# A triangular solve moved into the attention of a hybrid layer, and its successor's preparation spread over the projections

## The chip, the cores and the metric

The kernel runs on one core of one Trainium2 chip. The metric is the device time of one execution in microseconds (us). A core has several engines, each with its own queue of instructions, which meet through semaphores: TensorE (PE; its weight loads are listed as PEld), VectorE (DVE), ScalarE (ACT), GpSimd (POOL) and SyncE (SP), which here issues the DMAs.

## The reference, cut to what matters

One layer of a diffusion backbone over 512 latent tokens with 256 context tokens ahead of them, model width 1024, in float32. One input projection feeds two branches: softmax attention (8 query heads, 2 key heads) and a bidirectional chunked gated DeltaNet (8 heads, two directions, chunks of 64). The branches are gated, merged and projected; a gated MLP with a short convolution follows. The change concerns the triangular solve of the DeltaNet branch:

```python
gam = jnp.cumsum(log_a, axis=-1)
dec = jnp.exp(jnp.where(incl, gam[..., :, None] - gam[..., None, :], -jnp.inf))
kk = jnp.einsum('bhncd,bhnsd->bhncs', k, k)
a_mat = jnp.where(strict, beta[..., :, None] * dec * kk, 0.0) + jnp.eye(GDN_CHUNK)
uw = lax.linalg.triangular_solve(a_mat, rhs, left_side=True, lower=True, unit_diagonal=True)
...
def step(s, inp):
    delta = u_c - jnp.einsum('bhcd,bhde->bhce', w_c, s)
    s_new = gl_c[..., None, None] * s + jnp.einsum('bhcd,bhce->bhde', kd_c, delta)
    o = jnp.einsum('bhcd,bhde->bhce', qd_c, s) + jnp.einsum('bhcs,bhse->bhce', p_c, delta)
```

## The kernel before

Activations lie transposed, channels on the 128 partitions and tokens along the free axis. Every projection is a float32 product built from three matmuls: a weight block of 128 x 1024 is loaded (`wraw`), split into a high part on ACT (`whi`) and the rest on DVE (`wlo`), and multiplied with the high and low parts of the activations (`hxH`, `hxL` for latent tokens, `hcH`, `hcL` for context). The sums stand in two PSUM banks (`mb`); a third bank (`xb`) serves transposes, a pair (`ab`) and a large bank (`pS`) the attention.

The stages in the order of the trace: modulation vectors (to 50 us), key, value and query projections (to 153), attention (to 325), fill steps with the first DeltaNet pair's preparation and solve (to 428), the stages of the four DeltaNet pairs with their scans (to about 800), then gated merge, output projection and MLP (to the end), in which PE has hardly a pause.

*Attention.* `attend()` runs 32 units (8 heads x 4 blocks of 128 queries) plus two to drain. A unit takes scores, softmax, transposes of the probabilities, and the product with the values. Between its parts it takes steps of `fillA`, the projections of the DeltaNet's keys and values for the first heads; each of their results passes through the short convolution (taps on DVE into `t`, then `co`, an ACT tanh and a DVE product), is transposed through `xb`, scaled by `hk`, and stored to DRAM as `kTd`, `ktd` or `vtd`. The normalising factors of a head, `rkk` and `hk`, end in a power taken on POOL.

*DeltaNet pairs.* The 8 heads go in four pairs p = 0 to 3. `gdn_prep(p)` loads the keys `kT`, broadcasts `gamdr` into the decay tiles `NN` and `Gb`, adds the mask, takes 24 Exps on ACT (one per chunk, direction and head) and adds the two directions. `gdn_solve` multiplies these with the grams of the keys (PE into the single bank `pk`), gathers the 32 x 32 diagonal blocks into `C` (DVE transposes and ACT copies), turns them into `X`, and solves all blocks at once in 31 rows of two operations, a product `prod` and an addition to `R`. `gdn_solved` scales R by the rates `gT` and transposes it into `o_tr` and `o_nt`. `gdn_inv(p)` builds the full inverses from these on PE, and `gdn_scan(p)` does the recurrence. For p = 0 the 31 rows run on DVE, for the others on POOL.

*What sets the order.* From the attention's end on, PE's instructions stand in the order of the code (pinned); the other engines' instructions are placed by a scheduler with priorities (`sooner`, `solver`, `first`, `early`). `filler()` yields steps of projection work, and `weave(g, rate)` takes so many of them for each step of g. The code ahead of the first scan is 24 fill steps (`WK`), the first solve, 66 fill steps (`W0`), and the inverses with 2.4 fill steps to each of theirs:

```python
weave(wait(WK), 1.0)
weave(gdn_solve(pre, G if 0 in SPOOL else V), RK)
gdn_solved(pre, False)
weave(wait(W0), 1.0)
```

Helpers record most operations: in the profile L86 is a matmul, L90 a transpose on PE, L107 a tensor-tensor operation, L111 a tensor-scalar one, L116 a scalar-tensor-tensor one, L119 an activation.

Of the kernel before, what the change touches and what calls it, by code (L numbers as in the profile page):

```python
# [6 lines left out]
F32 = mybir.dt.float32  # L7
F32R = mybir.dt.float32r
AF = mybir.ActivationFunctionType
ALU = mybir.AluOpType  # L10
# [21 lines left out]
CHUNK, WK, W0, W1, RI, RS, RO = 1, 24, 66, 0, 3.0, 2.8, 2.0  # L32
# [45 lines left out]
def hybrid_layer_body(tc, x, ctxt, xT, consts, cols, rows, w_mod1, w_mod2, w_av, w_aq, w_cm, w_pa, w_pd, w_out,  # L78
# [26 lines left out]

    def tt(out, a, b, op, eng=None):
        (eng or V).tensor_tensor(out=out, in0=a, in1=b, op=op)  # L107

    def ts(out, a, s1, op0, s2=None, op1=None, eng=None):
        if op1 is None:  # L110
            (eng or V).tensor_scalar(out=out, in0=a, scalar1=s1, scalar2=None, op0=op0)  # L111
        else:
            (eng or V).tensor_scalar(out=out, in0=a, scalar1=s1, scalar2=s2, op0=op0, op1=op1)  # L113

    def stt(out, a, s, b, op0, op1):
        V.scalar_tensor_tensor(out=out, in0=a, scalar=s, in1=b, op0=op0, op1=op1)  # L116

    def act(out, a, f=AF.Copy, **kw):
        A.activation(out, a, f, **kw)  # L119
# [13 lines left out]
    with es:  # L133
# [89 lines left out]
        vtd = [dp.tile([P, NA], F32, name=f"vtd{i}") for i in range(NH)]  # L223
        szd = [dp.tile([P, NL], F32, name=f"szd{i}") for i in range(NH)]
# [445 lines left out]
        QH = [ap_.tile([P, 2, NL], F32R, name=f"QH{i}") for i in range(4)]  # L670
        QL = [ap_.tile([P, 2, NL], F32R, name=f"QL{i}") for i in range(4)]
# [90 lines left out]
        with at_es:  # L762
# [62 lines left out]

            def attend():
                U = 4 * NH
                at = lambda u: (u // 4, u % 4)
                pS, pms, pv = scores(0, 0), {}, None
                yield F0  # L830
                for u in range(U + 2):
                    if u < U:
                        pms[u] = softmax(*at(u), pS)
                    if u + 1 < U:
                        pS = scores(*at(u + 1))
                    yield F1
# [40 lines left out]
        def gdn_prep(p, eng=G):  # L877
# [25 lines left out]
            return [kT, gT, NN]  # L903

# [292 lines left out]

        with early():
            pre = gdn_prep(0, V if P0 else G)
# [3 lines left out]
        def filler():  # L1203
# [95 lines left out]
        count = [0.0]  # L1299

        def weave(g, rate):
            for w in g:
                count[0] += rate * (w or 1)
                while count[0] >= 1.0:
                    count[0] -= 1.0
                    next(fill, None)
# [14 lines left out]
        weave(gdn_solve(pre, G if 0 in SPOOL else V), RK)  # L1321
        gdn_solved(pre, False)
# [8 lines left out]
        for p in range(NP):  # L1331
            cur = pre
            pre = gdn_prep(p + 1) if p + 1 < NP else None
            g = stage(p, cur, pre)
            weave(g, RI if p else RI0)
            while not gpool or len(ready) < 2 * p + 2:
                next(fill)
# [273 lines left out]
```

## Time and profile before

| | us |
|---|---|
| median of three runs | 1258.49 |
| the three runs | 1258.39, 1258.49, 1265.28 |
| the profiled execution | 1256.38 |
| its span in the trace | 1254.5 |

The profiled execution's time is 1.9 over its span. The profile gives it in 40 slices of 31 us; each digit is the busy share in tenths:

```profile
PE   7999999999889899899999999899999999999996
DVE  5767767777698866766757687855776766653333
ACT  6634466766675673773634632233544444442231
POOL 0120110110422387597484200210000000000000
```

The attention ends in the eleventh slice. POOL has little to do up to there; in the three or four slices behind it DVE and ACT are at their fullest and PE falls to 8. The rest of the profile is read in the prediction.

### The profile page before, as it was taken

The numbers are of one execution on the slowest core, as the hardware profiler recorded it, in microseconds if no ns is written. First come the engines' busy times: TensorE is split into PE (matmuls) and PEld (weight loads), VectorE is DVE, ScalarE is ACT, GpSimd is POOL, SyncE is SP. The second block draws the span as 40 slices with busy tenths as digits, with TensorE's granted clock in tenths as the row PEclk, the third lists the DMA queues.
The fourth block names the chain that finished last, engine by engine and source line by source line (L and its number), as shares of the span: only waits on it lengthen the run. The fifth ranks groups of instructions, "written<-read, shape, count | busy, mean of one in ns | idle before, by whom it ended". The sixth has DMA issues, their size and how long they took to land. (4 is left out here: it accounts for less than half of the span.)

```text
span 1254.5 us, 20509 instructions
## 1 busy us (share of the span) xinstructions
PE 1196.7 (95%) x7733; PEld 1018.3 (81%) x7733; DVE 837.4 (67%) x1609; ACT 613.8 (49%) x1403; POOL 274.0 (22%) x347
## 2 busy tenths in 40 slices
PE   7999999999889899899999999899999999999996
PEld 3599879898778788778888778679888888888886
DVE  5767767777698866766757687855776766653333
ACT  6634466766675673773634632233544444442231
POOL 0120110110422387597484200210000000000000
PEclk9999999999999999999999999999999999999999
DMA  9412311211634533643546786854343332233331
GB/s 377 145 60 85 103 43 60 80 68 60 214 110 162 179 119 115 171 140 107 174 143 192 239 295 210 272 194 135 96 136 122 133 101 101 88 93 96 102 93 67
DMA packets 66403, 171.83 MB, mean 137 GB/s; under 512 B 7328, under 2 KB 18048, under 8 KB 64896
## 3 DMA queue, kind: packets, MB, share of 16 engines
q1 hardware_dynamic: 66304, 170.52, 41.0%
q8 instruction: 61, 1.00, 0.3%
q14 instruction: 38, 0.31, 0.1%
HBM read 145.28 MB, written 25.21 MB: 136 GB/s over the span
## 5 line engine op out<-in xcount | busy, mean ns | idle before, releaser
L107 DVE TENSOR_TENSOR wlo<-wraw,whi 128x1024 fp32r<-128x1024 f32 (+1 forms) x153 | 192.2, 1257 | 155.7 <-ACT whi L119 155.5
L119 ACT ACTIVATE whi<-wraw 128x1024 fp32r<-128x1024 f32 (+1 forms) x153 | 159.6, 1044 | 219.3 <-PE mc L86 112.5
L86 PE MATMUL mc<-h,whi 128*128 128x512 f32 (+1 forms) x752 | 219.7, 376 | 0.3 <-ACT whi L119 0.3
L86 PE MATMUL mb<-hxH,whi 128*128 128x512 f32 x384 | 162.3, 423 | 3.4 <-DVE R L107 2.8
L86 PEld LDWEIGHTS mc<-h,whi 128*128 128x128 f32 x752 | 138.0, 188 | 25.8 <-ACT whi L119 0.5
L86 PE MATMUL mb<-hxH,wlo 128*128 128x512 f32 x384 | 152.6, 397 | 0.0
L86 PE MATMUL mb<-hxL,whi 128*128 128x512 f32 x384 | 151.7, 395 | 0.0
L86 PE MATMUL mc<-h,wlo 128*128 128x512 f32 (+1 forms) x376 | 141.4, 376 | 0.5 <-DVE wlo L107 0.5
L86 PE MATMUL mc<-a,whi 128*128 128x512 f32 (+1 forms) x396 | 111.1, 367 | 0.6 <-DVE x L116 0.6
L107 POOL TENSOR_TENSOR rc<-rc,mhalf 128x2 f32<-128x2 f32 x4 | 3.3, 813 | 407.5 <-DVE rc L113 407.5
L86 PEld LDWEIGHTS mb<-hxH,wlo 128*128 128x128 f32 x384 | 72.9, 190 | 16.5
L86 PEld LDWEIGHTS mb<-hxH,whi 128*128 128x128 f32 x384 | 73.5, 191 | 13.7 <-issue 2.9
L86 PEld LDWEIGHTS mc<-h,wlo 128*128 128x128 f32 x376 | 70.8, 188 | 13.8 <-DVE wlo L107 1.0
L86 PEld LDWEIGHTS mc<-a,whi 128*128 128x128 f32 x396 | 71.6, 189 | 12.8 <-DVE x L116 0.8
L86 PEld LDWEIGHTS mb<-hxL,whi 128*128 128x128 f32 x384 | 73.5, 191 | 9.6
L86 PE MATMUL mc<-a,wlo 128*128 128x512 f32 (+1 forms) x198 | 72.4, 366 | 0.0
L116 DVE SCALAR_TENSOR_TENSOR u<-mc,col,u 128x511 f32<-128x511 f32 x88 | 65.3, 746 | 1.4
L107 POOL TENSOR_TENSOR prod<-X,R 128x31 f32<-128x31 f32 (+15 forms) x93 | 54.4, 584 | 20.6 <-DVE X L107 13.9
L107 POOL TENSOR_TENSOR R<-R,prod 128x31 f32<-128x31 f32 (+15 forms) x93 | 57.1, 614 | 7.0
L86 PE MATMUL pq<-whi,hxH 128*128 128x256 f32 (+1 forms) x192 | 55.6, 290 | 0.0
L86 PE MATMUL pq<-wlo,hxH 128*128 128x256 f32 (+1 forms) x192 | 54.4, 283 | 0.1
L86 PE MATMUL pq<-whi,hxL 128*128 128x256 f32 (+1 forms) x192 | 54.3, 283 | 0.0
(329 smaller groups left out, 2768.1 us busy)
## 6 DMA issues: line engine op xcount, KB each, us to landing
wraw<-in_w_cm_dram SPq DMA_DIRECT2D x48, 512.0 KB, 3.6
wraw<-in_w_up_dram SPq DMA_DIRECT2D x44, 512.0 KB, 3.3
wl<-in_w_mod_dram SPq DMA_DIRECT2D x24, 512.0 KB, 4.6
wm<-in_w_mod_dram SPq DMA_DIRECT2D x8, 1024.0 KB, 10.7
wraw<-in_w_down_dram SPq DMA_DIRECT2D x16, 512.0 KB, 3.5
wraw<-in_w_aq_dram SPq DMA_DIRECT2D x10, 512.0 KB, 3.7
M<-gamdr SPq DMA_DIRECT2D x64, 64.0 KB, 4.9
wraw<-in_w_pa_dram SPq DMA_DIRECT2D x8, 512.0 KB, 4.4
```

What stands on the lines that cost most here:

```text
L86: i = nc.tensor.matmul(*a, **k)
L107: (eng or V).tensor_tensor(out=out, in0=a, in1=b, op=op)
L116: V.scalar_tensor_tensor(out=out, in0=a, scalar=s, in1=b, op0=op0, op1=op1)
L119: A.activation(out, a, f, **kw)
```

## The change

The first pair's masks, decays, grams, blocks and solve are taken out of the code behind the attention and cut into pieces. A generator `first_solve()` yields them, and `solve_pieces(u)`, called in each unit of the attention, takes pieces worth one credit a unit (`S0R`), none before the unit that a piece names. All of a piece's instructions are pinned into the program's order on their engines (`in_order`, `put`). The 31 rows stand in unit 20 with no credit, on POOL; the scaling by gT stands in unit 32, on POOL too. The tiles take the places of query tiles that are no longer needed (QH and QL become one tag `Q` with four buffers), so the results go to DRAM: `nnd` (the masked grams) and `rrd` (R). `gdn_first()` loads them again, with kT.

Behind the attention there are 8 fill steps (`WK`), the two transposes `o_tr` and `o_nt` (pinned), 12 fill steps (`W0`), and the first pair's inverses. The second pair's preparation and solve become `gdn_pieces(1)`, cut in the same way; `side_pieces` takes from them half a credit (`SRA`) with each fill step. Its masks and rows are on POOL. The fill steps take the query and z projections of two heads as q, q, z, z in place of q, z, q, z. The number of matmuls is unchanged.

```diff
-CHUNK, WK, W0, W1, RI, RS, RO = 1, 24, 66, 0, 3.0, 2.8, 2.0
+S0E, S0R, SRA = 0, 1, .5
+CHUNK, WK, W0, W1, RI, RS, RO = 1, 8, 12, 0, 3.0, 2.8, 2.0
...
+    def put(i):
+        return tc.keep_in_program_order(i) if strict[0] else i
...
-        QH = [ap_.tile([P, 2, NL], F32R, name=f"QH{i}") for i in range(4)]
-        QL = [ap_.tile([P, 2, NL], F32R, name=f"QL{i}") for i in range(4)]
+        QQ = [ap_.tile([P, 2, 2, NL], F32R, name="Q", tag="Q", bufs=4) for _ in range(4)]
+        QH, QL = ([q[:, i] for q in QQ] for i in range(2))
...
+                def masks(D, d, hh):
+                    tc.keep_in_program_order(SP.dma_start(
+                        D.rearrange("p a b -> p (a b)"),
+                        gamdr[rows6(d, hh), :].rearrange("a b -> (a b)").partition_broadcast(P)))
+                    tt(D, D, msk_s[d].unsqueeze(1).to_broadcast([P, 6, P]), ALU.add, G)
...
+                def gram(hh, c0, n):
+                    pb = xbank()
+                    for i in range(n):
+                        sl = slice((c0 + i) * P, (c0 + i + 1) * P)
+                        mm(pb[:, i, :], kT[hh][:, sl], kT[hh][:, sl])
+                    tt(NN[hh][:, c0:c0 + n, :], NN[hh][:, c0:c0 + n, :], pb[:, 0:n, :], ALU.mult)
...
+                def row(j):
+                    m, n = 31 - j, j + 1
+                    pv = Gb.rearrange("p a b -> p (a b)")[:, 0:m * n].rearrange("p (i k) -> p i k", k=n)
+                    tt(pv, X[0][:, j, j + 1:32].unsqueeze(2).to_broadcast([P, m, n]),
+                       R[0][:, j:j + 1, 0:n].to_broadcast([P, m, n]), ALU.mult, G)
+                    tt(R[0][:, j + 1:32, 0:n], R[0][:, j + 1:32, 0:n], pv, ALU.add, G)
...
+                def spill():
+                    for hh in range(2):
+                        SP.dma_start(nnd[hh], NN[hh].rearrange("p a b -> p (a b)"))
+
+                def close():
+                    tt(R[0], R[0], gT.unsqueeze(2).to_broadcast([P, 32, 32]), ALU.mult, G)
+                    SP.dma_start(rrd, R[0].rearrange("p a b -> p (a b)"))
+
+                E = S0E
+                yield E, 0, lambda: masks(NN[0], 0, 0)
+                yield E, 0, lambda: masks(Gb, 1, 0)
+                yield E, 1, lambda: None
+                for D, d in ((NN[0], 0), (Gb, 1)):
+                    for c in (0, 2, 4):
+                        yield E + 1, 1, lambda: decay(D, d, 0, c)
+                yield 0, 0, lambda: tt(NN[0], NN[0], Gb, ALU.add, G)
+                yield 7, 0, more
+                yield 7, 0, lambda: masks(Gb, 1, 1)
+                yield 7, 0, lambda: masks(NN[1], 0, 1)
+                yield 7, .5, lambda: gram(0, 0, 4)
+                yield 7, .5, lambda: gram(0, 4, 2)
+                yield 7, 0, lambda: load(1)
...
+                        yield 15, .5, lambda: blocks(b, hh)
+                yield 0, 0, spill
+                yield 0, .5, turn
+                yield 0, .5, scale
+                for j in range(31):
+                    yield 0, 0, lambda: row(j)
+                yield 32, 0, close
...
         with early():
-            pre = gdn_prep(0, V if P0 else G)
+            pre = gdn_first()
...
-            for h in range(NH):
-                yield from head_proj(h, 0)
-                ready.append(h)
-                yield from z_proj(h)
+            for h in range(0, NH, 2):
+                for i in range(2):
+                    yield from head_proj(h + i, 0)
+                    ready.append(h + i)
+                for i in range(2):
+                    yield from z_proj(h + i)
...
-        weave(gdn_solve(pre, G if 0 in SPOOL else V), RK)
-        gdn_solved(pre, False)
+        gdn_solved(pre, True, 1)
+        second = []
+        side[0] = gdn_pieces(1, second)
         weave(wait(W0), 1.0)
```

Three places show how instructions move. In each row stand the line of the program, the operation, and what it writes and reads; numbers behind the names tell tiles apart.

The first is PE in the attention where unit 8's scores (`pS`) are taken. Before, a projection (`mb`) follows at once:

```order
L86 MATMUL pS_2387<-KH_717,QH1_723 128x512
L86 MATMUL pS_2387<-KL_718,QH1_723 128x512
L86 MATMUL pS_2387<-KH_717,QL1_727 128x512
L86 MATMUL pS_2387<-KH_717,QH1_723 128x256
L86 MATMUL pS_2387<-KL_718,QH1_723 128x256
L86 MATMUL pS_2387<-KH_717,QL1_727 128x256
L86 MATMUL mb_2407<-hxH_196,whi_2401 128x512
```

In the changed kernel (`sA` holds the keys of head 0 in the place of a query tile):

```order
L87 MATMUL pS_2405<-KH_720,Q_726 128x512
L87 MATMUL pS_2405<-KL_721,Q_726 128x512
L87 MATMUL pS_2405<-KH_720,Q_726 128x512
L87 MATMUL pS_2405<-KH_720,Q_726 128x256
L87 MATMUL pS_2405<-KL_721,Q_726 128x256
L87 MATMUL pS_2405<-KH_720,Q_726 128x256
L87 MATMUL xb_2419<-sA_2413 128x128 x4
L87 MATMUL xb_2425<-sA_2413 128x128 x2
L87 MATMUL mb_2442<-hxH_199,whi_2436 128x512
```

Six gram matmuls in two groups, both through `xb`, now stand between the scores and the projection.

The second is DVE at the attention's end (`PL` is the low part of the last probabilities, `gwh` a constant). Before, the rates `g` of the pairs come behind it:

```order
L107 TENSOR_TENSOR PL_3810<-ab_3843,PH_3809 128x4x128
L116 SCALAR_TENSOR_TENSOR co_3576<-co_3576,t1_3583 128x768
L107 TENSOR_TENSOR PL_3810<-ab_3850,PH_3809 128x2x128
L111 TENSOR_SCALAR gwh_3895<-col_74 128x1
L883 MEMSET g_3900 128x8
L116 SCALAR_TENSOR_TENSOR g_3900<-beta_159,rkk0_177 128x6
L116 SCALAR_TENSOR_TENSOR g_3900<-beta_159,rkk1_178 128x6
```

In the changed kernel the two transposes of R come there, ahead of the taps (`t1`) of the first projection behind the attention:

```order
L119 TENSOR_TENSOR PL_3965<-ab_4007,PH_3964 128x2x128
L123 TENSOR_SCALAR gwh_4052<-col_74 128x1
L1191 STREAM_TRANSPOSE o_tr_4107<-R_4056 128x32x32
L1191 STREAM_TRANSPOSE o_nt_4108<-R_4056 128x32x32
L128 SCALAR_TENSOR_TENSOR t1_4069<-mb_4070,col_74,t1_4069 128x511 x2
L119 TENSOR_TENSOR wlo_4565<-wraw_4563,whi_4564 128x1024
L128 SCALAR_TENSOR_TENSOR t1_4069<-mb_4114,col_74,t1_4069 128x255 x2
L128 SCALAR_TENSOR_TENSOR co_4062<-co_4062,t1_4069 128x768
```

R_4056 comes from DRAM by a load on SP, behind the store of `sB`, which holds R in the attention:

```order
L360 DMA kTd5_116<-co_3731 128x768
L917 DMA rrd_145<-sB_2935 128x1024
L824 DMA atd7_161<-ao_3847 128x512
L1441 DMA R_4056<-rrd_145 128x1024
L1443 DMA NN_4055<-nnd0_143 128x768
L1444 DMA kT_4054<-kTd0_111 128x768
```

The store stands behind the scaling of R on POOL, and that behind the factors of head 4:

```order
L119 TENSOR_TENSOR sB_2935<-sB_2935,Gb0_1989 128x31
L119 TENSOR_TENSOR rkk4_184<-rkk4_184,mhalf_78 128x6
L119 TENSOR_TENSOR hk4_171<-hk4_171,col_74 128x6
L119 TENSOR_TENSOR sB_2935<-sB_2935,gs0_1990 128x1024
L1006 MEMSET TTm_4048 128x3072
```

The third is ACT some 35 us behind the attention, where the second pair's last decays are taken (`Gb_4208`; `NN_5690` belongs to the third pair, `TTm` to the inverses of the first). Before, the first pair's decays and the second's stand there with nothing of the inverses:

```order
L119 ACTIVATE NN_3912<-NN_3912,gam_160 128x128 x6
L119 ACTIVATE co_3949<-t1_3956 128x768
L119 ACTIVATE NN_4747<-NN_4747,gam_160 128x128 x6
L119 ACTIVATE t1_4045<-mb_4046,col_74 128x512
L119 ACTIVATE NN_4747<-NN_4747,gam_160 128x128 x6
L119 ACTIVATE co_4081<-xb_4082,hk4_168 128x128 x4
L119 ACTIVATE Gb_3931<-Gb_3931,gam_160 128x128 x6
```

In the changed kernel:

```order
L131 ACTIVATE NN_5690<-NN_5690,gam_163 128x128
L131 ACTIVATE t1_4399<-mb_4473,col_74 128x256
L131 ACTIVATE NN_5690<-NN_5690,gam_163 128x128 x7
L131 ACTIVATE TTm_4048<-pb_4540 64x6x64
L131 ACTIVATE TTm_4048<-pb_4541 64x6x64
L131 ACTIVATE NN_5690<-NN_5690,gam_163 128x128 x4
L131 ACTIVATE co_4480<-xb_4577,hk5_172 128x128 x2
L131 ACTIVATE Gb_4208<-Gb_4208,gam_163 128x128 x3
```

Twelve Exps of the third pair now stand ahead of the second pair's last six.

More of the change, by code (lines that the diff above doesn't have):

```diff
@@ L223, in hybrid_layer_body @@
         vtd = [dp.tile([P, NA], F32, name=f"vtd{i}") for i in range(NH)]
+        nnd = [dp.tile([P, 6 * P], F32, name=f"nnd{i}") for i in range(2)]
+        rrd = dp.tile([P, D], F32, name="rrd")
         szd = [dp.tile([P, NL], F32, name=f"szd{i}") for i in range(NH)]
@@ L826, in attend, with solve_pieces @@
+            fs_, fnext = first_solve(), []
+            def solve_pieces(u):
+                left = S0R
+                while left > 0:
+                    if not fnext:
+                        fnext.append(next(fs_, None))
+                    if fnext[0] is None or fnext[0][0] > u:
+                        return
+                    left -= fnext[0][1]
+                    in_order(fnext.pop()[2])
             def attend():
@@ L1299, in hybrid_layer_body, with side_pieces, fill_step @@
         count = [0.0]
+        side, due = [None], [0.0]
+        def side_pieces(credit):
+            due[0] -= credit
+            while side[0] is not None and due[0] <= 0:
+                share, fn = next(side[0], (0, None))
+                if fn is None:
+                    side[0] = None
+                else:
+                    in_order(fn)
+                    due[0] += share
+        def fill_step():
+            next(fill, None)
+            side_pieces(SRA)
         def weave(g, rate):
@@ L1305, in weave @@
                     count[0] -= 1.0
-                    next(fill, None)
+                    fill_step()
         def both(a, b):
@@ L1332, in hybrid_layer_body @@
             cur = pre
-            pre = gdn_prep(p + 1) if p + 1 < NP else None
-            g = stage(p, cur, pre)
-            weave(g, RI if p else RI0)
+            if p == 0:
+                pre = second
+                weave(gdn_inv(p, cur), RI0)
+            else:
+                pre = gdn_prep(p + 1) if p + 1 < NP else None
+                weave(stage(p, cur, pre), RI)
             while not gpool or len(ready) < 2 * p + 2:
-                next(fill)
+                fill_step()
+            side_pieces(99)
             g = gdn_scan(p, cur, gdn_load(p), pre)
```

165 lines of the change are left out of this document (160 added, 5 removed).

## The prediction

> **What bounds the kernel now.** I read the page's totals, then the busy time by stage, then PE's waits in the one stage where the change takes work away, then the granted clock there.
>
> ```profile
> span 1254.5 us, 20509 instructions
> PE 1196.7 (95%) x7733; PEld 1018.3 (81%) x7733; DVE 837.4 (67%) x1609; ACT 613.8 (49%) x1403; POOL 274.0 (22%) x347
> ```
>
> PE is busy 1196.7 of 1254.5 us. Only the 57.8 us in which it idles, and the time in which it runs at a lower clock, can be won. By stage (columns: us, then busy time of each engine, granted PE clock, DMA share, GB/s):
>
> ```profile
> 153.00:325.40 172.40, 167.56 (x1117) 150.25 (x1118) 126.23 (x251) 110.52 (x282) 16.70 (x12) 0.98 0.19 69
> 325.40:428.00 102.60, 88.70 (x646) 75.14 (x645) 86.37 (x170) 70.62 (x196) 40.46 (x35) 0.93 0.52 169
> 428.00:511.00 83.00, 77.53 (x532) 65.96 (x530) 59.46 (x113) 45.95 (x127) 58.18 (x82) 1.00 0.45 146
> 511.00:700.00 189.00, 185.80 (x1744) 159.54 (x1744) 125.78 (x249) 105.08 (x280) 122.65 (x182) 0.99 0.47 149
> ```
>
> The first row is the attention (PE idle 4.8), the second the fill steps with the first pair's preparation and solve: PE idles 13.9 of 102.6 us, DVE is 84% busy, and the clock is 0.93. What PE waits for in that second row (us in total, times, longest):
>
> ```profile
> PE xb L90 <- DVE co L116: 6.0, 3, 2.9
> PE mb L86 <- DVE R L107: 2.8, 1, 2.8
> PE xb L90 <- ACT co L119: 1.7, 1, 1.7
> PE pb L86 <- DVE gT L890: 1.5, 1, 1.5
> PE pb L86 <- DVE o_tr L952: 1.1, 1, 1.1
> PE mb L86 <- DVE t L116: 0.6, 2, 0.5
> ```
>
> They add to 13.7. A longer wait also costs clock. One of near 3 us ends at 344.2; the three windows of 3.4 us around it, in the columns above:
>
> ```profile
> 340.60:344.00 3.40, 0.69 (x6) 0.49 (x5) 2.79 (x2) 3.40 (x12) 2.77 (x2) 1.00 0.53 164
> 344.00:347.40 3.40, 3.16 (x15) 3.17 (x16) 2.15 (x4) 3.40 (x13) 0.00 (x0) 0.50 0.09 31
> 347.40:350.80 3.40, 3.31 (x25) 2.84 (x25) 1.82 (x3) 3.03 (x8) 0.00 (x0) 1.00 0.00 0
> ```
>
> Behind the wait the clock is 0.50 for 3.4 us: 15 matmuls, then 25 at full clock. Half of 3.4 us, 1.7 us, is lost again. Over the stage (1 - 0.93) x 102.6 = 7.2 us. So the stage holds 13.7 + 7.2 = 20.9 us, 1.7% of the span, and that is the most the change can win there. The Trainium skill, "TensorE: Matmul & The Clock Gate", Part 1, says the clock halves after an idle window of about 3.4 us. By that rule a wait of 2.9 us would cost its 2.9 us alone; the row shows the half clock behind it, and only the length of the window agrees.
>
> **The change, part by part.** The profiled execution spans 1254.5 and takes 1256.38; the median of the runs is 1258.49, 2.1 more. I sum against the execution and add the 2.1.
>
> *Taken away: the rows on DVE behind the attention.*
>
> ```profile
> L107 DVE TENSOR_TENSOR R<-R,prod 128x31 f32<-128x31 f32 (+15 forms) x31 | 15.1, 486 | 0.6
> L107 DVE TENSOR_TENSOR prod<-X,R 128x31 f32<-128x31 f32 (+15 forms) x31 | 11.4, 368 | 0.6
> L107 POOL TENSOR_TENSOR R<-R,prod 128x31 f32<-128x31 f32 (+15 forms) x31 | 18.5, 597 | 2.4
> L107 POOL TENSOR_TENSOR prod<-X,R 128x31 f32<-128x31 f32 (+15 forms) x31 | 17.9, 578 | 16.3 <-DVE X L107 13.9
> ```
>
> DVE loses 26.5 us; POOL (last two rows: the second pair's solve, 628 to 670 us) needs 36.4 plus gaps, some 41 us, for the same 62 operations. From unit 20 on there are 12 units of 5.05 us (172.4 us for the 34 steps of the loop), 61 us: the rows end before the attention does. The waits on R, gT and o_tr (5.4) go with the rows. Those on co need a second look:
>
> ```profile
> 339.69 1.85 ACT L119 ACTIVATE NN<-NN,gam 128x128 f32<-128x128 f32 x6
> 341.45 0.83 ACT L119 ACTIVATE co<-t 128x768 f32<-128x768 f32 x1
> 342.31 1.87 DVE L116 SCALAR_TENSOR_TENSOR co<-co,t 128x768 f32<-128x768 f32 x1 [0.61 <-ACT co L119]
> 344.24 1.11 PE L90 MATMUL xb<-cst,co 128*128 128x128 f32 x4 [2.94 <-DVE co L116]
> ```
>
> ACT's six Exps (1.85) stand ahead of co's tanh, which ends at 342.28; DVE then takes 1.87. The longest co wait is due to Exps, not to rows, and as many Exps stay in this stage (pairs 1 and 2 in place of 0 and 1, 24 each). I keep one such wait, 2.9 us, of the 7.7.
>
> *Added in the attention, unit 7.* The first head's grams run as 4 + 2 matmuls, with nothing between, in the only xbank, behind the load of kT.
>
> ```profile
> 194.60 0.32 SPq L314 DMA_DIRECT2D vtd<-co  x1
> 196.87 0.39 PE L86 MATMUL mb<-hxH,whi 128*128 128x512 f32 x1
> 198.10 1.22 DVE L107 TENSOR_TENSOR wlo<-wraw,whi 128x1024 fp32r<-128x1024 f32 x1
> DMA to landing us min/median/max: 3.2/6.0/8.8
> L107 DVE TENSOR_TENSOR NN<-NN,pk 128x512 f32<-128x512 f32 (+1 forms) x5 | 2.9, 579 | 2.6 <-PE pk L86 2.6
> ```
>
> The load follows the vtd store (first row) on SP: 194.9, landing after 3.2 at best (fourth row: loads of kT), 198.1; PE is there at 196.9, so 1.2 us. The second gram waits for DVE's product (0.6) of the first, behind wlo (1.22): 1.5 more. Together 2.7, and 1.7 for the clock. The second head's two grams have other matmuls between them; 0.6 each, and 0.6 for the rest: 6.2 us. Ends: 1 (load and wlo early) and 10 (landing at the median). ACT gets 24 Exps of 0.31 and 8 block copies, DVE products and block transposes; with 110.5 and 126.2 busy of 172.4 they have room.
>
> *At the attention's end.* The result goes POOL, DRAM, back, DVE.
>
> ```profile
> 319.61 0.33 ACT L119 ACTIVATE rkk<-gkss,col 128x6 f32<-128x6 f32 x1
> 321.31 1.31 POOL L107 TENSOR_TENSOR hk<-hk,col 128x6 f32<-128x6 f32 x1
> L107 POOL TENSOR_TENSOR NN<-NN,Gb 128x768 f32<-128x768 f32 x2 | 3.7, 1841 | 6.0 <-ACT Gb L119 6.0
> kTd<-co SPq DMA_DIRECT2D x4, 384.0 KB, 2.3
> L952 DVE STREAM_TRANSPOSE o_tr<-R 128x1024 f32<-128x1024 f32 x1 | 2.0, 2005 | 0.0
> 337.22 0.39 PE L86 MATMUL mb<-hxL,whi 128*128 128x512 f32 x1
> 337.45 0.39 PE L86 MATMUL mb<-hxH,wlo 128*128 128x512 f32 x1
> 340.78 0.28 PE L86 MATMUL mb<-hcH,whi 128*128 128x256 f32 x1
> 340.90 0.28 PE L86 MATMUL mb<-hcL,whi 128*128 128x256 f32 x1
> ```
>
> With T = 325.4: POOL must do rkk and hk of head 4, whose input comes at 319.9; hk ends at 322.6, T - 2.8. R x gT has 1024 columns against 768 (1.84): 2.5, so T - 0.3. The store lands 2.3 later (as kTd), T + 2.0. The load of R takes 3.2 to 6.0; it is first of its bunch, I take 3.8: T + 5.8. DVE's two transposes, pinned ahead of the taps, take 2.0 each, the taps 1.5: T + 11.3. PE meanwhile does 24 matmuls at 0.23, 24 at 0.12 and 6 more, 9.0 us, and then needs the bank those taps empty: 2.3 late, with the clock 4.0. Ends 0 and 6. Behind the waiting transposes stand wlo and both taps; behind the store on SP only loads that are not yet needed.
>
> *The second pair's last gram.* Its product waits for the POOL sum behind Gb's six Exps, and these now stand on ACT behind twelve hoisted Exps of the third pair. The gram's own bank is single. The trace has no such order; the nearest row is the wait above that Exps ahead of co made, 2.9, plus 1.7: 4.6. Ends 0 (covered by the matmuls of the fill step) and 9 (all eighteen Exps, 5.6, and a product, late, with the clock twice).
>
> Scan 0 starts earlier, with the same matmuls in all; that by itself gains nothing where PE is the bound. Sum: -20.9 + 2.9 + 6.2 + 4.0 + 4.6 = -3.2. 1256.4 - 3.2 = 1253.2 in the execution, with 2.1 some **1255 us**.
>
> **Rivals.**
> - *All new waits hidden* (kT lands early, banks last): only the R round trip stays, -20.9 + 4.0 = -16.9, 1242. For it: the waits taken away are measured, the new ones are estimates. Against: the grams stand back to back in PE's order.
> - *New waits without the half clock*: gaps of 2.3 to 2.9 do not always halve it. Three times 1.7 less: 1250. Against it is the row at 344.0. It is what the rule cited above from the Trainium skill, taken literally, would give.
> - *DVE late in the attention, so slower*: DVE's co took 1.87 at 342.31 while POOL was busy. For eight units, with POOL without a pause, the operations with two SBUF inputs can stretch so. DVE has 126.2 of 172.4 busy, 3.7 of each unit; wlo and co (0.6 a unit) and the pieces (0.5) doubled make 5.2 to 5.4 of 5.05. From where a unit passes 5.05 it decides: eight units x 0.3 = 2.4, with the clock three times 5.1, and the late grams at their upper ends (4 + 4): 1255 + 13 = 1268. The Trainium skill, "GPSIMD Engine Reference", section 8, has GpSimd share its SBUF interfaces with VectorE, against DVE instructions with two SBUF inputs; the trace agrees with 1.87. Against its full weight: the rows are small, mostly under 256 columns.
> - *The move does nothing*: the Exps set all the co waits and the third pair's Exps the rest: 7.7 + 3 of clock stay besides the new ones: 1258 to 1262.
>
> **Numbers.** Forecast 0.42 (1249 to 1261), all hidden 0.20 (1238 to 1247), no half clock 0.10 (1246 to 1254), DVE late 0.15 (1261 to 1276), nothing 0.13. About 1%, 12.6 us, is what a measurement of this kernel can tell from no change: below 1245.9 lies most of the second case and a little of the third, 0.20; above 1271.1 a part of the fourth, with slips I have no price for, 0.09; between 0.71. The range 1243 to 1267 leaves out 0.1 on each side.
>
> **What would show it.** Right: in the stage behind the attention no waits on R, gT and o_tr, the clock above 0.97, a PE gap near T + 9 on the taps behind o_tr, and gaps at the grams of unit 7. Wrong: attention units longer than 5.05 us with PE waiting on DVE (fourth case), or PE idle under 5 us from T to the first scan (second). If the total falls by more than 21 us, time was won in a stage for which I gave nothing.

## The result, and the profile after

The changed kernel takes 1275.02 us (median of four runs, 1272.97 to 1278.18) against 1259.32 before (four runs by now). The ratio is 1.0117, 95% interval 1.0078 to 1.0156: slower by about 1.2%. The forecast was 1255, with a range of 1243 to 1267. Medians here and below leave out two executions that were slow as a whole, one of e1 with 4166.68 us, its profiled one, and one of e2 with 4507.61.

The page of the changed kernel's profile, its span and the busy time by engine:

```profile
span 1271.2 us, 20538 instructions
PE 1198.4 (94%) x7733; PEld 1020.4 (80%) x7733; DVE 811.5 (64%) x1544; ACT 615.6 (48%) x1407; POOL 320.9 (25%) x416
```

DVE has lost 25.9 us of work and POOL has gained 46.9, as intended; PE's busy time is 1.7 us more. By stage (attention; from its end to the first scan; from there to the gated merge; columns as before):

```profile
155.60:343.80 188.20, 173.34 (x1139) 153.36 (x1140) 141.24 (x270) 122.28 (x314) 67.00 (x83) 0.98 0.24 79
343.80:440.00 96.20, 80.59 (x697) 67.64 (x696) 52.96 (x91) 67.69 (x184) 60.05 (x62) 0.96 0.56 181
440.00:728.20 288.20, 277.98 (x2351) 239.65 (x2349) 184.26 (x375) 151.82 (x408) 157.91 (x235) 0.98 0.44 143
```

The lengths can't be compared as they are, because fill steps have moved between the stages. So I use PE's *loss*: the length of a stretch less the sum, over its matmuls, of the median distance that a matmul of that shape has to its successor in the trace before. It contains waits and half clock, and leaves out work that moved. (The values of the table are rounded each by itself.)

| stretch | length before | loss before | length after | loss after | change |
|---|---|---|---|---|---|
| to the first scores | 153.6 | 17.0 | 155.6 | 19.0 | +2.0 |
| attention | 171.6 | 10.4 | 188.2 | 24.4 | +13.9 |
| to the first scan | 120.0 | 25.1 | 96.1 | 23.1 | -2.0 |
| to the gated merge | 256.7 | 22.5 | 288.2 | 27.3 | +4.8 |
| to the end | 545.7 | 21.4 | 536.2 | 19.3 | -2.1 |
| sum | | 96.4 | | 113.1 | +16.7 |

The first row is ahead of the change, and the profiles of the runs further down scatter there by as much (16.7 to 19.0). A loss from one trace contains chance: where the granted clock is halved, it is so for a period of 3.41 us, worth 1.7, and the same instructions have such a period in one run and not in another (unit 7 below). In the attention this cancels, with two periods in the trace before and two after. The attention holds most of the loss: 16.6 us longer, of which 2.7 are the first pair's grams, moved in from behind. Cut at the starts of the scores, its steps compare one to one with those before (step n runs from the nth scores to the next, beside the pieces of unit n - 2). The step with the first head's grams takes 11.97 in place of 5.92; seven steps from the sixteenth to the twenty-second are 1.8, 0.5, 1.0, 0.0, 0.6, 1.2 and 2.5 longer; the fourth is 1.2 longer; and the last nine, beside GpSimd's rows, differ by 0.1 at most. PE's waits in the attention (us in total, times, longest; the wait for qsc was there before, and so were 2.7 of the 3.1 for xb):

```profile
PE pS L87 <- ACT pm L131: 4.5, 4, 2.3
PE xb L91 <- ACT xb L131: 3.1, 3, 1.3
PE pS L87 <- DVE qsc L125: 3.0, 1, 3.0
PE xb L87 <- DMA sA<-kTd: 1.8, 1, 1.8
...
PE xb L87 <- DVE NN L119: 0.8, 1, 0.8
```

And from the attention's end to the first scan:

```profile
PE pk L87 <- DVE NN L119: 4.8, 1, 4.8
PE xb L91 <- ACT co L131: 4.3, 1, 4.3
PE mb L87 <- DVE t L128: 3.2, 2, 2.8
PE xb L91 <- ACT xb L131: 1.8, 1, 1.8
PE xb L91 <- DVE co L128: 1.5, 1, 1.5
```

The waits on R, gT and o_tr are gone, but 15.6 us of others stand in place of 13.7. From the first scan to the gated merge the two longest:

```profile
PE pb L87 <- DVE oacc L119: 5.2, 2, 3.5
PE xb L91 <- ACT xb L131: 3.6, 1, 3.6
```

There the waits add to 9.9 in place of 8.2, but the clock is halved in four periods, from 501.0, 535.2, 596.6 and 688.8, where before it was in one, from 511.3: three more are 5.1 us, as much as this stage lost.

**The grams of unit 7.** The load of the keys is issued at 198.65. The two grams, and the clock behind them:

```profile
202.43 1.16 PE L87 MATMUL xb<-sA 128*128 128x128 f32 x8 [1.79 <-DMA sA<-kTd]
203.69 0.69 DVE L119 TENSOR_TENSOR NN<-NN,xb 128x512 f32<-128x512 f32 x1 [0.46 <-issue]
204.43 1.22 PE L87 MATMUL xb<-sA 128*128 128x128 f32 x4 [0.84 <-DVE NN L119]
200.66:204.07 3.41, 1.16 (x8) 0.97 (x8) 2.94 (x5) 0.94 (x2) 0.38 (x1) 1.00 1.06 262
204.07:207.48 3.41, 3.05 (x11) 2.66 (x12) 3.38 (x6) 1.76 (x5) 3.12 (x2) 0.50 0.82 201
```

PE waits 1.8 for the load and 0.8 for the first gram's bank, and half of the clock is missing for 3.4 us, 1.7. The 1.7 is chance: e4, e9 and e12 below keep these pieces as they are and have waits of 1.4 and 0.8 there, but the clock stays at 1.00, and their step is 4.2 us longer and not 6.0.

**A small DVE piece in the softmax chain.** Around the scaling of X by gT in unit 20:

```profile
277.99 1.22 DVE L119 TENSOR_TENSOR sB<-sB,gs 128x1024 f32<-128x1024 f32 x1
279.13 0.95 DVE L128 SCALAR_TENSOR_TENSOR co<-co,t 128x768 f32<-128x768 f32 x1
280.00 0.95 DVE L832 TENSOR_REDUCE mx<-pS 128x1 f32<-128x768 f32 x1
281.79 0.15 DVE L128 SCALAR_TENSOR_TENSOR mx<-mx,qsc 128x1 f32<-128x1 f32 x1
281.84 1.14 ACT L131 ACTIVATE co<-xb,hk 128x128 f32<-128x128 f32 x4 [1.22 <-POOL Gb L119]
282.86 1.01 ACT L131 ACTIVATE pm<-pS,mx,qsc 128x768 f32<-128x768 f32 x1
284.01 0.50 PE L87 MATMUL pS<-KH,Q 128*128 128x512 f32 x1 [2.26 <-ACT pm L131]
```

The scaling holds up co, co the maximum, and the maximum the Exp pm, which then finds co's evacuation ahead of it on ACT; the next scores need pS empty. 1.2 us on an engine that is 75% busy costs PE 2.3. That the profile names a row on GpSimd (`Gb`) as what released co's evacuation is chance: PE's transposes into xb end at 281.76, and e5 below, without rows, has this long step too.

**The second pair's last gram and the load of R**, both priced in the prediction:

```profile
382.66 2.71 POOL L119 TENSOR_TENSOR Gb<-Gb,cst 128x768 f32<-128x768 f32 x1
386.97 0.98 ACT L131 ACTIVATE Gb<-Gb,gam 128x128 f32<-128x128 f32 x3
387.85 0.83 ACT L131 ACTIVATE co<-t 128x768 f32<-128x768 f32 x1
388.58 0.97 ACT L131 ACTIVATE Gb<-Gb,gam 128x128 f32<-128x128 f32 x3
389.69 1.80 POOL L119 TENSOR_TENSOR NN<-NN,Gb 128x768 f32<-128x768 f32 x1 [4.33 <-ACT Gb L131]
391.53 0.69 DVE L119 TENSOR_TENSOR NN<-NN,pk 128x512 f32<-128x512 f32 x1 [1.86 <-POOL NN L119]
392.27 1.22 PE L87 MATMUL pk<-kT 128*128 128x128 f32 x4 [4.76 <-DVE NN L119]
392.30:395.70 3.40, 3.40 (x12) 2.94 (x13) 2.12 (x3) 0.91 (x1) 0.62 (x1) 0.57 0.36 116
```

```profile
347.18 0.32 SPq L1441 DMA_DIRECT2D R<-rrd  x1
350.78 2.06 DVE L1191 STREAM_TRANSPOSE o_tr<-R 128x1024 f32<-128x1024 f32 x1 [6.49 <-DMA R<-rrd]
354.50 1.52 DVE L128 SCALAR_TENSOR_TENSOR t<-mb,col,t 128x511 f32<-128x511 f32 x2
356.07 0.50 PE L87 MATMUL mb<-hxH,whi 128*128 128x512 f32 x1 [2.82 <-DVE t L128]
350.84:354.25 3.41, 2.42 (x20) 2.05 (x18) 3.41 (x2) 1.80 (x6) 1.17 (x3) 1.00 1.02 357
354.25:357.67 3.42, 1.59 (x7) 1.33 (x8) 2.54 (x4) 3.09 (x9) 2.85 (x6) 1.00 1.05 366
```

The first gram's chain is a mask on POOL, Exps, co's tanh between them, a POOL sum, the product; PE stands 4.8 us and runs at 0.57 for 3.4 us. The mask of Gb ends at 385.4, so the third pair's hoisted Exps ahead of Gb's on ACT hold these up by 1.6 us at most. R's load, two transposes, taps, and PE 2.8 us late with its clock at 1.00.

### The profile page after: what moved, and what is told of

Read it like the earlier page. It is cut to its first block, busy times and chain, and to the rows that moved or that the text cites. A ratio compares the mean times of both kernels' runs of the same rounds, so it can differ in the third digit from the quotient of the medians.

```text
span 1271.2 us, 20538 instructions
## 1 busy us (share of the span) xinstructions
PE 1198.4 (94%) x7733; PEld 1020.4 (80%) x7733; DVE 811.5 (64%) x1544; ACT 615.6 (48%) x1407; POOL 320.9 (25%) x416
## 5 line engine op out<-in xcount | busy, mean ns | idle before, releaser
L119 DVE TENSOR_TENSOR wlo<-wraw,whi 128x1024 fp32r<-128x1024 f32 (+1 forms) x153 | 189.2, 1237 | 164.2 <-ACT whi L131 159.6
L87 PE MATMUL mb<-hxH,whi 128*128 128x512 f32 x384 | 165.7, 431 | 3.2 <-DVE t L128 3.2
L87 PEld LDWEIGHTS mc<-h,whi 128*128 128x128 f32 x752 | 138.0, 188 | 25.9 <-ACT whi L131 0.5
L87 PE MATMUL mb<-hxL,whi 128*128 128x512 f32 x384 | 153.6, 400 | 0.0
L87 PEld LDWEIGHTS mc<-h,wlo 128*128 128x128 f32 x376 | 70.8, 188 | 13.8 <-DVE wlo L119 1.0
```

Of the source, the lines that this page charges most:

```text
L87: i = nc.tensor.matmul(*a, **k)
L119: put((eng or V).tensor_tensor(out=out, in0=a, in1=b, op=op))
```

## The experiments

Ratios are to the kernel before, with 95% intervals. A loss is that of the kernel's profiled execution, from one trace.

**One half of the change alone.**

```diff
# e1, from the changed kernel
-        side[0] = gdn_pieces(1, second)
+        side[0] = None
...
-            if p == 0:
-                pre = second
-                weave(gdn_inv(p, cur), RI0)
-            else:
-                pre = gdn_prep(p + 1) if p + 1 < NP else None
-                weave(stage(p, cur, pre), RI)
+            pre = gdn_prep(p + 1) if p + 1 < NP else None
+            weave(stage(p, cur, pre), RI if p else RI0)
# e2, from the changed kernel
-CHUNK, WK, W0, W1, RI, RS, RO = 1, 8, 12, 0, 3.0, 2.8, 2.0
+CHUNK, WK, W0, W1, RI, RS, RO = 1, 24, 66, 0, 3.0, 2.8, 2.0
...
-                    solve_pieces(u)
...
-            pre = gdn_first()
+            pre = gdn_prep(0, V if P0 else G)
...
-        gdn_solved(pre, True, 1)
+        weave(gdn_solve(pre, V), RK)
+        gdn_solved(pre, False)
```

> The second pair's preparation and solve go back to their places (prepared in one go, solved in the stage of the first pair); the first pair's solve stays in the attention. Theory A (the pieces in the attention hold PE: it was 188.2 us long in place of 171.6): the attention stays at 187 to 189 us and the total at 1266 to 1276, less than the changed kernel by at most the wait on the second pair's gram, 4.8 us and some 1.5 of clock. Theory B (the second pair's pieces behind the attention are what costs): 1262 or less.

> The first pair is prepared and solved on DVE behind the attention as before, with 24 and 66 fill steps; only the second pair's pieces stay. Theory A: the attention is back at 171 to 172 us and the total at 1255 to 1263. Theory B: 1268 or more, with the loss behind the attention.

e1 took 1281.32, ratio 1.0163 [1.0129, 1.0196], more than the changed kernel and than either theory said. It has no trace of an ordinary execution; that with 8 and 12 fill steps the second pair's preparation has too little beside it is only argued. e2 took 1264.80, 1.0038 [1.0017, 1.0058]: the attention is back, 170.4 us, step for step as before, so its loss comes from the first pair's pieces. Yet the total is above the kernel before; up to the first scan the loss is 34.9 in place of 25.1, with one long row among PE's waits:

```profile
PE pk L87 <- DVE NN L119: 15.0, 3, 7.9
```

The two longest, 7.9 and 4.1, are before pinned grams of the second pair; the third, 3.1, is before one of the first pair's own. Each half costs by itself.

**The pieces in the attention**, each from the changed kernel.

```diff
# e3: first head's grams later
-                yield 7, .5, lambda: gram(0, 0, 4)
-                yield 7, .5, lambda: gram(0, 4, 2)
+                yield 9, 1, lambda: gram(0, 0, 4)
+                yield 10, 1, lambda: gram(0, 4, 2)
# e4: block copies on GpSimd
-                    act(C[sb, :, 6 * hh:6 * hh + 6], NN[hh][sb, :, sb].rearrange("p u j -> p j u"))
+                    put(G.tensor_copy(C[sb, :, 6 * hh:6 * hh + 6], NN[hh][sb, :, sb].rearrange("p u j -> p j u")))
# e5: no rows, store of R earlier
-                for j in range(31):
-                    yield 0, 0, lambda: row(j)
-                yield 32, 0, close
+                yield 29, 0, close
```

> The first head's two grams are moved from unit 7 to units 9 and 10, the load of its keys stays in unit 7. Theory A1 (the step with the two grams took 11.97 us in place of 5.92 because they wait for the load of the keys and for each other's bank): that step falls to 6 to 7 us, two later steps gain some 0.7 each for the matmuls, total 1269 to 1272. Rival A2 (any gram in the attention's single transpose bank stops PE, wherever it stands): the loss moves with the grams, total 1274 to 1277.

> The eight block copies of the first pair go from ACT to POOL, which is idle there. Theory A3 (PE waits for ACT's softmax and transposes behind these copies in units 15 to 21, whose steps are 7.5 us longer than before in all): 3 to 5 us come back, total 1269 to 1272. Rival A4 (the DVE pieces there do it: block transposes, the turn, the scaling, 1.2 us each): no change, 1274 to 1277.

> The 31 rows of the first pair's solve are left out (R stays the unit matrix), so GpSimd is idle where they ran, and the scaling and the store of R are moved up to unit 29. Theory C0 (the rows on GpSimd cost the attention nothing): the steps from unit 22 on are as long as before either way, and the attention stays at 186 to 189 us. Rival C1 (GpSimd's rows slow VectorE): the attention is 3 us or more shorter. The store moved up: the R load is issued near the attention's end instead of 3.4 us behind it, and PE's wait on the taps behind o_tr, 2.8 us, falls to 0.5 or less.

e3: 1269.53, 1.0073 [1.0045, 1.0101]. The long step is 6.0, three later ones gain 0.6, 0.9 and 0.9, and the attention's loss falls from 24.4 to 19.5. A1 holds. e4: 1273.09, 1.0114 [1.0074, 1.0153], not told apart from the changed kernel. Steps 16 to 22 are 5.1 longer than before in place of 7.5: the copies on ACT held 2.4 of it, less than A3's 3 to 5. The step of 2.5 stays at 2.4, and PE's wait there is again on ACT's pm, 2.3, as A4 has it: DVE's pieces begin that chain. e5: 1272.96, 1.0112 [1.0063, 1.0160]. The last nine steps, the same instructions of PE and DVE, first beside the rows (changed kernel), then without:

```profile
284.01:330.60 46.59, 46.59 (x318) 42.31 (x319) 37.48 (x70) 28.94 (x67) 33.91 (x53) 1.00 0.17 60
284.98:331.48 46.50, 46.50 (x318) 42.25 (x319) 35.21 (x70) 28.80 (x67) 0.00 (x0) 1.00 0.17 61
```

With POOL busy 33.9 of 46.6 us, the same 70 DVE instructions take 2.3 us more, and PE loses 0.1. C0 holds: the rows themselves were free. What did cost PE beside GpSimd in the changed kernel is the one large operation behind them, the scaling of R:

```profile
340.12 1.91 POOL L119 TENSOR_TENSOR sB<-sB,gs 128x1024 f32<-128x1024 f32 x1
340.77 2.08 DVE L128 SCALAR_TENSOR_TENSOR co<-co,t 128x768 f32<-128x768 f32 x1
```

DVE's co takes 2.08 there and 0.96 in the trace before, PE waits 0.8 behind it, and the part behind the last scores is 1.1 longer; in e5, where the scaling comes earlier, it is as long as before. The earlier store did not help: R's load was issued 1.1 us behind the attention's end and not 3.4, but its data were there only 5.5 us later, and PE's wait was 2.5 in place of 2.8.

**All edits at once, and a later scan.** e6 takes e3 and e4, puts the second head's grams in two units, the scaling on GpSimd, and the second pair's last grams six fill steps later; e7 also has the store earlier and 40 fill steps in place of 12.

```diff
# e6, besides e3 and e4
-                    tt(X[0], X[0], gT.unsqueeze(2).to_broadcast([P, 32, 32]), ALU.mult)
+                    tt(X[0], X[0], gT.unsqueeze(2).to_broadcast([P, 32, 32]), ALU.mult, G)
...
-                yield 0, .5, lambda: gram(1, 0, 4)
-                yield 0, .5, lambda: gram(1, 4, 2)
+                yield 0, 1, lambda: gram(1, 0, 4)
+                yield 0, 1, lambda: gram(1, 4, 2)
...
             for hh in range(2):
+                if hh:
+                    yield 3, lambda: None
```

> All edits that the trace names at once: first head's grams in units 9 and 10, second head's in two units, block copies and the scaling of X on GpSimd, and in the fill steps the second pair's second head's grams six steps later. Theory A (the pieces stand in front of the softmax chain and of the transposes) expects the attention at 178 to 181 us, the pk wait (4.8 and 1.5 of clock) gone, total 1260 to 1265. Rival D (PE is given work that ends its slack anywhere in the attention): attention 184 or more, total 1268 or more.

> As the kernel with all edits spread out, with the store of R moved up to unit 29 and 40 fill steps in place of 12 ahead of the first pair's inverses, so that the second pair's rows on GpSimd are over when the first scan's masks M come there. Theory E (ACT waits for M, and co and PE behind it, 4.3 us and 1.6 of clock, because M's additions stand behind the rows): that wait goes and the total is 5 to 9 below the kernel with all edits spread out, 1253 to 1259. Rival F (another wait takes its place, since as many Exps and additions have to pass ACT and GpSimd beside the same projections): within 3 of it.

e6: 1266.12, 1.0063 [1.0042, 1.0083], just over the expected 1260 to 1265, with the attention at 184.9: that is D's sign (184 or more), while the total lies between the two theories. With the scaling on GpSimd the step behind the turn (DVE's transpose that makes X) is as before (0.1), and the turn's own step is 1.8 longer. In e3, with both on DVE, these two steps are 0.6 and 1.0 longer, in the changed kernel 1.2 and 2.5: the price of the same 1.2 us on DVE depends on the unit in which it falls. The pk wait is gone, but DVE's t (4.4) and ACT's t (3.2) take its place. e7: 1271.14, 1.0091 [1.0061, 1.0122]: the wait on ACT's co is down to 1.0, and the total is 5 us more than e6, not less. That is rival F's way, and more than its 3: DVE's t (5.2) and the pk wait (3.0) stand there instead.

**What ACT and GpSimd carry behind the attention.** e8 leaves out the second pair's Exps, e9 its rows.

> The second pair's 24 Exps among the fill steps are left out (its mask additions become a multiplication by zero on GpSimd, so its grams are masked to zero); all else as in the changed kernel. Theory G (behind the attention ACT's Exps stand in front of the evacuations that PE waits for): of PE's waits from the attention's end to the first gated merge, 25.5 us, the pk wait of 4.8 and the co waits of 5.8 go, total 1262 to 1268. Rival H (the waits come from GpSimd's and DVE's pieces): 20 us or more of waits stay, total 1271 to 1277.

> The second pair's 31 rows on GpSimd are left out (its R stays the unit matrix); all else as in the changed kernel. Theory E (the first scan's masks M stand behind these rows on GpSimd, ACT behind M, co and PE behind ACT): the wait on co of 4.3 us near 436 and the half clock behind it go, total 1266 to 1270. Rival (M is late because its loads are): the wait stays at 3 us or more, 1272 to 1277.

e8: 1267.55, 1.0081 [1.0060, 1.0103]. The loss to the first scan falls from 23.1 to 13.8, the pk wait to 0.2 and the co wait to 0.8: G is right in that stage. But from there to the merge the loss is 32.4 in place of 27.3, 1.7 of the difference being clock. e9: 1270.46, 1.0097 [1.0063, 1.0131]; the wait on ACT's co falls from 4.3 to 1.5, and the stage behind loses 30.1 in place of 27.3. Theory E has its mechanism; its 1266 to 1270 is just missed.

**Only the rows gone from behind the attention.**

```diff
# e10: e3, e4, the attention's edits of e6, the store of R in unit 29; behind it as before
-CHUNK, WK, W0, W1, RI, RS, RO = 1, 8, 12, 0, 3.0, 2.8, 2.0
+CHUNK, WK, W0, W1, RI, RS, RO = 1, 24, 66, 0, 3.0, 2.8, 2.0
...
# e11: e10 with the old order of projections; e12: the changed kernel with it
-            for h in range(0, NH, 2):
-                for i in range(2):
-                    yield from head_proj(h + i, 0)
-                    ready.append(h + i)
-                for i in range(2):
-                    yield from z_proj(h + i)
+            for h in range(NH):
+                yield from head_proj(h, 0)
+                ready.append(h)
+                yield from z_proj(h)
```

> The first pair's solve stays in the attention with its pieces spread out; behind the attention everything is as before, 24 and 66 fill steps, the second pair prepared in one go and solved in the first pair's stage. So the only thing that is new behind the attention is that DVE's rows are gone from it and R is loaded. My prediction's term (the waits on R, gT and o_tr go, most of the clock with them): PE's waits from the attention's end to the first gated merge fall from 21.9 us to 14 or less and the loss there from 47.5 to 38 or less, total 1255 to 1261. Rival I (the Exps and evacuations in ACT's order set them anyway): waits of 18 or more, total 1265 to 1272.

> As the kernel with the fill as before, and the fill steps' projections in the old order too (q, z, q, z). There the stage behind the attention gained what the prediction had in its term (PE's waits to the first scan 6.1 us in place of 13.7, the loss 11.3 in place of 25.1), but the stages from the first scan to the gated merge lost 11 more than before. Theory J (the order q, q, z, z made that loss): PE's loss from the first scan on falls by 8 or more and the total is 1253 to 1259, at or under the time before. Rival K (the waits only moved: the same evacuations and pieces meet the first scan in another place): 1262 to 1268.

> The changed kernel with the old order of the projections (q, z, q, z) and nothing else undone. Theory J: 5 us or more below the changed kernel, 1265 to 1270. Rival K: 1272 to 1278.

e10: 1265.43, 1.0043 [1.0021, 1.0064]. Its waits from the attention's end to the first scan, all of them, and that stretch's window, behind it the one of the kernel before:

```profile
PE xb L91 <- DVE co L128: 5.3, 3, 3.0
PE xb L91 <- ACT co L131: 0.8, 1, 0.8
339.20:440.10 100.90, 94.82 (x773) 80.27 (x772) 58.51 (x100) 69.13 (x189) 45.56 (x38) 0.98 0.58 191
325.20:445.20 120.00, 106.10 (x809) 89.19 (x808) 99.58 (x188) 82.02 (x223) 45.74 (x40) 0.94 0.51 168
```

The loss is 11.3 in place of 25.1, the clock 0.98 in place of 0.94. The waits on co stay, with no row on DVE. Ahead of the longest stand six Exps on ACT (1.87) and the copies of R's transposes (2.1); that the Exps make it is argued here, and shown by e8 for the changed kernel alone. From the first scan to the merge the loss is 33.9 (22.5 before), so over both stages the waits are 20.7 and the loss 45.2: rival I's numbers, though in the first stage the prediction's term is there. e11: 1266.76, 1.0059 [1.0037, 1.0081], with 11.1 and 30.1 in these two stages; e12: 1272.18, 1.0117 [1.0092, 1.0142]. The order of the projections changes nothing; J falls. (The trace of e10 is of its longest run, 1269.10, that of e11 of its shortest, 1261.97.) From the first scan on, PE's instructions in e11 are those of the kernel before with the fill steps shifted by four, which the solve behind the attention had taken; it gets to the scan 8.1 us earlier, and is 6.1 us later at the MLP's first matmul (837.9 and 831.8).

**A shift alone, and the rows on GpSimd without the attention.**

```diff
# e13, from the kernel before
-CHUNK, WK, W0, W1, RI, RS, RO = 1, 24, 66, 0, 3.0, 2.8, 2.0
+CHUNK, WK, W0, W1, RI, RS, RO = 1, 28, 60, 0, 3.0, 2.8, 2.0
# e15, from the kernel before: the pairs whose rows run on GpSimd
# (e16: e15 with 82 or 90 in place of 66 for W0)
-SPOOL = [int(c) for c in '123']
+SPOOL = [int(c) for c in '0123']
```

> The kernel before with the same work, and only the fill steps around the first solve shifted: 28 ahead of it and 60 behind it in place of 24 and 66. Nothing is moved between engines. Theory L (the stages from the first scan on are sensitive to where the other engines' instructions fall, since only PE's order is fixed; a shift alone costs there): 1261 or more. Rival M (a shift of two to four steps changes nothing beyond the runs' spread): 1256 to 1260.

> The kernel before with one letter changed: the first pair's 31 rows run on GpSimd where they stand, behind the attention, in place of VectorE. Nothing is added to the attention and nothing goes through DRAM. Theory N (what the stage behind the attention gains is VectorE's freedom from the rows, 14 us of PE's loss in the kernel with the fill as before): the loss from the attention's end to the first scan falls from 25 to 11 to 18, total 1248 to 1257. Rival I (the gain is given back behind the first scan as there): 1257 to 1263.

> The first pair's rows on GpSimd where they stand, with 82 fill steps behind them in place of 66, so that PE reaches the inverses some 16 us later: the wait of 14.6 us on o_tr that this kernel showed with 66 should be gone. If nothing else moves: 1269.7 - 14.6 - 1.7 = 1253. If the shift costs from the first scan on as in the shifted kernel before: 1258 to 1263.

> The same with 90 fill steps: no wait on o_tr, 1253 if nothing else moves, 1258 to 1263 if the shift costs as in the shifted kernel before. The two together show how much a shift alone scatters.

e13: 1266.79, 1.0048 [1.0020, 1.0077]. Nothing but fill steps moved, and it costs 7.5 us; from the first scan to the merge the loss is 29.4 in place of 22.5, and 5.1 of these 6.9 are three more periods of half clock. (This trace is of a run of 1268.45, 12.1 over the one before, so some of that is the run's own.) The price that theory L gave is there. e15: 1269.71, 1.0089 [1.0060, 1.0118]; its longest wait to the first scan:

```profile
PE pb L86 <- DVE o_tr L952: 14.6, 1, 14.6
```

The rows on GpSimd, interleaved with masks, end too late for the inverses; co's waits, 5.9, are as ever. Both ranges expected, 1248 to 1257 and 1257 to 1263, are missed. With 82 and 90 steps the total is 1279.81, 1.0155 [1.0129, 1.0181], and 1271.35, 1.0089 [1.0065, 1.0112], both over the expected 1253 or 1258 to 1263. With 82 a wait of 4.8 on o_tr is left. With 90 the wait on o_tr is gone, and the loss from the first scan to the merge is 17.8, but from the merge to the MLP it is 40.5 in place of 15.7: which fits that the steps spent early are missing late. PE's two longest waits there (merge to MLP, 90 steps):

```profile
PE pb L90 <- DVE oacc L111: 5.6, 1, 5.6
PE mb L86 <- DVE at L107: 5.0, 1, 5.0
```

No version ran faster than the kernel before.

## Why the prediction was wrong

The sum forecast -3.2, and the trace shows +16.7. Of the 19.9 between, 7.7 lie in the attention, 7.4 in the stage behind it (-9.4 forecast, -2.0 measured) and 4.8 between the first scan and the merge.

The first step that failed is the attention's term. I put it at 6.2 us; its loss grew by 13.9. Unit 7 came in size: 2.7 of waits and 1.7 of clock forecast, 2.6 and 1.7 measured. Part of that is luck. The load cost 1.8 and not 1.2, the bank 0.8 and not 1.5, for DVE's product did not stand behind wlo, which had ended at 202.8; and the 1.7 of clock comes in some runs only. What failed is the rest, "0.6 each, and 0.6 for the rest", 1.8 us, with the sentence that ACT and DVE "have room" at 110.5 and 126.2 busy of 172.4. The measured rest is 9.6. The steps with the second head's grams, the block transposes, the turn and the scaling lost 6.2 of it (7.6 less the grams' 1.4), the fourth step, behind the first Exps, 1.2, and the end beside the scaling of R 1.1. Room on an average is not room in the chain: between two scores PE needs the maximum, the Exp and the evacuations in one order, and a pinned piece delays all behind it. e2 (attention restored), e3 (grams), e4 (the copies 2.4) and e6 (the scaling) show this; how the rest divides among the block transposes and the turn is open, since none of these was taken out alone.

The gain behind the attention was sized about right and not kept. My terms there gave -20.9 + 2.9 = -18.0 for the rows; e10, with the rows alone gone, measured -13.8. Most of the difference is co: I kept 2.9 of its 7.7, and 6.1 stayed. The load of R (2.3 and 1.7 forecast) was 2.8 with no half clock, since both windows around it show 1.00. The second pair's gram (2.9 and 1.7) was 4.8 and 1.5, at a clock of 0.57 over 3.4 us; of the 4.8, the hoisted Exps named for it explain 1.6 at most. But the changed kernel also has ACT's co behind the scan's masks and two more evacuations, 7.6 us of waits together where I kept 2.9, and its stage gained 2.0 in all.

What was missing altogether is the stages from the first scan on, for which I wrote that an earlier start "by that itself gains nothing". It loses: 4.8 here, 7.6 to 11.4 in e11 and e10, of which two or three more periods of half clock are 3.4 to 5.1. e13 shows that most of this does not need the change: a shift of fill steps, with the same work on every engine, lost 6.9 there. The shift changes which fill matmuls stand between the scan's own, and the scheduler places DVE's, ACT's and GpSimd's instructions anew; the waits that follow are on oacc, r and xb. Which of the two makes them was not tried, so theory L is shown as a price of a shift and not by its mechanism.

Of the rivals, DVE late came nearest in time (1268), with units that passed their 5.05 us through DVE. But it named the units beside GpSimd's rows, and those kept their length; e5 refutes the rows as the cause. The Trainium skill, "GPSIMD Engine Reference", section 8, names this contention; here it was 2.3 us of DVE's time beside the rows, 0.1 of PE's, and 1.1 of the attention at its end, beside one operation of 1024 columns. It was the small pinned pieces and not the large moved one.

Of the four signs for being right, three came: no waits on R, gT and o_tr, a gap at 353.3 (T + 9.5, with the attention's end now at 343.8) on the taps behind o_tr, and gaps in unit 7. The clock was 0.96 and not above 0.97. None of them looks at the steps in which the attention lost the rest.

## What to carry to other kernels

An engine's average busy share says nothing about a loop in which a chain over three engines just fits: price a piece put there by what stands behind it in that chain, step by step, not by idle time; the same piece can cost 0.6 us in one step and 1.8 in another. What is won ahead of a stage whose engines are placed by a scheduler must be measured at the end, and beside a run in which the same stage is only shifted; here such a shift cost 7.5 us, as much as the gains in question. Before moving work off an engine, ask which of the waits would stay without it: the co waits did, in every version that kept the Exps.

## What the runs showed of the hardware

The half clock does not follow from a wait's length alone: behind 2.8 us at 356.1 the clock stayed at 1.00, and behind 1.8 and 0.8 us at 202.4 and 204.4 it was 0.50. Where a wait falls matters too. In the changed kernel's trace the half periods begin at 204.07, 391.83, 501.05 and 535.2 among others, each a whole multiple of 3.41 us from the next: they lie on a fixed grid. In the grid window ahead of 204.07 PE was busy 1.16 of 3.41 us, and the next window had half clock. The wait at 356.1 fell across the border at 354.25, which left 2.42 and 1.59 busy on its two sides, and no half clock followed. The Trainium skill, "TensorE: Matmul & The Clock Gate", Part 1, calls the window that decides free-running; the trace agrees. The grid lies elsewhere in each run: e9 has the pieces of unit 7 with no half clock, and has one from 283.2, beside unit 20.

The load of R, 512 KB, was usable 5.5 us after its issue in e5, where it was issued 2.3 us earlier relative to the attention's end, and 3.6 us after it in the changed kernel. The early issue thus gained 0.4 us. Why it took longer is open.
